# A decoder trunk on one core: SwiGLU's seven products with the tokens stationary and the weights moving 512 wide, the gated product turned by VectorE and on-chip transfers

## The chip, the cores and the metric

The kernel runs on one core of a Trainium2 chip. That core has five engines with instruction streams of their own: TensorE (PE: matrix products, with weight loads listed apart as PEld), VectorE (DVE), ScalarE (ACT), GpSimd (POOL) and SyncE (SP, which here only issues transfers). Each engine runs its stream strictly in order and waits on semaphores for the others. The metric is device time in microseconds for one execution of the whole program; lower is better.

## The reference

The program computes two layers over 512 tokens of width 1024: a recurrent layer, then an attention layer, each followed by a SwiGLU of hidden width 2816. Only the two SwiGLUs are touched by the change:

```
def rms_norm(x, g):
    y = x32 * lax.rsqrt(jnp.mean(x32 * x32, axis=-1, keepdims=True) + EPS)
    return y * g
def swiglu(h, w_in, w_out):
    g, u = jnp.split(h @ w_in, 2, axis=-1)
    return (jax.nn.silu(g) * u) @ w_out
...
h = h + swiglu(rms_norm(h, a_ffn_norm[i]), a_ffn_w_in[i], a_ffn_w_out[i])
```

## The kernel before, in words

Every float32 operand of a product is held as two parts, `hi` (its rounded value) and `lo` (the rest), and one product is three matmuls: hi by hi, hi by lo, lo by hi (`mm3`, lines 183 to 187). ScalarE makes `hi` by a cast, VectorE makes `lo` by a subtraction. So each weight tile costs one cast on ScalarE and one subtraction on VectorE before TensorE can use it; these pairs are called splits below.

The residual stream `h` lies with channels on the partitions and the 512 tokens along the free axis, as eight tiles. A SwiGLU (`swiglu`, line 574) has 22 blocks of 128 hidden units for the gate and 22 for the up projection. N_PLAIN = 1 pair of blocks goes through plain products, 24 matmuls a block. The other 20 blocks go in ten pairs, `q` = 1 to 10, and each pair is done in seven products in place of eight, after Winograd: the input is cut into two halves of the channels and two of the tokens, sums of these are made once (`B11`, `B21`, `B22`, `T1` to `T4`), sums of the weight parts are made for every pair (`GA`, `GB`, `S1` to `S4`, `UB`), and product "S2.T2" multiplies weight sum S2 with token sum T2. `S1` and `S3` are summed by an accumulating transfer that POOL issues behind one that SP issues (lines 634 and 636), `S2` and `S4` by VectorE (lines 644 and 647). Results collect in three PSUM accumulators: GA, S2, S3 and UB add into the one that GA begins, S4 into the one that S1 begins, and GB has its own.

A product of a pair is 24 matmuls: a 128x128 weight block is the stationary operand, 256 tokens move, and the result has hidden units on the partitions. `gate` and `results` (lines 700 to 709) multiply with the norm's factors, apply Silu, multiply gate and up, and split the gated block into `gh` and `gl`, four hidden blocks in one chunk. A chunk has two buffers. It is used by the out product (`out_block`, line 746): step "O" of the order is 24 matmuls, 512 tokens wide, and VectorE subtracts the result from `h` (line 752). The last six hidden blocks go through a loop at the end (line 765), where each of the eight output blocks is finished, and `after` makes the next stage's input from it.

TensorE's order is written by hand, as the lists PRODUCTS and LAST_PRODUCTS (lines 41 and 42). The other engines' streams are put in order when the program is built, by a scheduler. The class `Stream` (line 90) hands out the weight tiles, called pieces: `get(i)` returns piece `i` and has the splits of the next two pieces and the loads of the next four written into the program (`asp`, `al`, line 575). Split tiles `wh` and `wl` have three buffers each, so the cast for a piece must wait until TensorE has read the piece three before it for the last time. Tiles as loaded, `wr`, have two buffers; the raw tiles of the seven products have N_RAW = 7 between them.

```
        hi = self.pool.tile([128, 1024], F32R, name=f"wh{i}", tag="wh")
        lo = self.pool.tile([128, 1024], F32R, name=f"wl{i}", tag="wl")
...
                nc.scalar.copy(hi[:, c], r[:, c])
                kind = self.pieces[i][1]
```

In a pair's steady state the order is S1, S2, GB, O, S3, GA of the next pair, S4, O, UB. Between GA of a pair and its S2, which adds into the same accumulator after ScalarE has copied GA's result out (line 732), stand S4, O and UB of the pair before and S1 of its own.

Of the kernel before, what the change touches and what calls it, by code (L numbers as in the profile page):

```python
# [39 lines left out]
N_PLAIN = 1  # L40
LAST_PRODUCTS = ["S1.T1", "S2.T2", "GB.B21", "S3.T3", "O", "S4.B22", "UB.T4"]
PRODUCTS = ["S1.T1", "S2.T2", "GB.B21", "O", "S3.T3", "GA.B11", "S4.B22", "O", "UB.T4"]
# [47 lines left out]
class Stream:  # L90
# [31 lines left out]
    def _split(self, i):  # L122
# [4 lines left out]
        if self.pieces[i][0] is None:  # L127
            return [lambda: self.pieces[i][1](hi, lo)]
# [44 lines left out]
def trunk(tc, A, out):  # L173
# [29 lines left out]
    class Ffn:  # L203


        def __init__(self, wi, wo, gain):
            self.gain = gain
            self.wi, self.wo = A[wi], A[wo]
            self.split = None
            self.marks = {}  # L210
            self.steps = []
            for j in range(2 * N_PLAIN):
                self.steps += [("plain", j, b, add_pieces([self.wi[b]])) for b in (j, HB + j)]
            waiting = []

            def product(q, name):
                pieces.append((None, lambda hi, lo: self.split(q, name, hi, lo)))
                self.steps.append(("product", q, name, len(pieces) - 1))

            product(N_PLAIN, "GA.B11")  # L220
            for q in range(N_PLAIN, HB // 2):
                if q % 2 == 0:
                    waiting += [(q // 2 - 1, m) for m in range(0, 8, 2)]
                out = 1 if q > HB // 2 - 3 else 2
                for name in PRODUCTS if q + 1 < HB // 2 else LAST_PRODUCTS:
                    if name == "GA.B11":
                        if q + 1 < HB // 2:
                            product(q + 1, name)
                    elif name != "O":
                        product(q, name)  # L230
                    elif out and waiting:
                        c, m = waiting.pop(0)
                        w = self.wo[m:m + 2, :, 512 * c:512 * c + 512].rearrange("b q c -> q b c")
                        self.steps.append(("out", c, m, add_pieces([w])))
                        out -= 1
            self.gated = [s[3] for s in self.steps if s[0] == "out"][:2]
            self.last = [add_pieces([self.wo[m][:, 128 * (HB - 6):128 * HB]]) for m in range(8)]

        def half(self, u, q, k):

            b = (HB if u else 0) + 2 * q
            return self.wi[b:b + 2, :, 512 * k:512 * k + 512].rearrange("b q c -> q b c")
# [7 lines left out]
    with tc.tile_pool(name="keep", bufs=1) as kp, tc.tile_pool(name="wts", bufs=3) as wp, \  # L250
# [82 lines left out]
        def norm_rows(pool, r, tag="sq", bufs=1, copy=S.copy, hold=None, low=None):  # L333
# [12 lines left out]
            rb = pool.tile([128, T], F32, name="rb", bufs=1)  # L346
# [226 lines left out]

        def swiglu(fp, p, after):
            ws.asp, ws.al = 2, 4

            def chunk(extra=""):
                return [fp.tile([128, 4, T], F32R, name=n, tag=n, bufs=2) for n in ("gh", "gl")]
# [3 lines left out]
            for n in ("T1", "T2", "T3"):  # L582
                homes[n] = [fp.tile([128, 4, 256], F32R, name=n + x, bufs=1) for x in "hl"]
# [43 lines left out]
            def raw(q, n):  # L627
                raws[q, n] = fp.tile([128, 2, 512], F32, name=n, tag="raw", bufs=N_RAW)
                return raws[q, n]

            def fetch(q, n):
                r = raws[q, n]
                u, k = {"GA": (0, 0), "GB": (0, 1), "S1": (1, 0), "S3": (0, 0), "UB": (1, 1)}[n]
                a = nc.sync.dma_start(r, p.half(u, q, k))
                if n in ("S1", "S3"):
                    nc.gpsimd.dma_start(r, p.half(1, q, n == "S1"), accum_op=ALU.add)  # L636
                return a

            def split_weights(q, name, hi, lo):
                n = name[:2]  # L640
                with tc.high_priority():
                    if n == "S2":
                        raws[q, n] = raws[q, "S1"]
                        V.tensor_tensor(raws[q, n], raws[q, n], raws[q, "GA"], ALU.add)
                    elif n == "S4":
                        raws[q, n] = raws[q, "GB"]
                        V.tensor_tensor(raws[q, n], raws[q, n], raws[q, "S2"], ALU.add)
                    r = raws[q, n].rearrange("q b c -> q (b c)")
                    S.copy(hi, r)  # L649
                    p.marks[q, n] = V.tensor_tensor(lo, r, hi.bitcast(F32), ALU.subtract)  # L650

            p.split = split_weights
            chunks, rows, plain, acc = {}, [], {}, {}

            def store(q, w, c=slice(0, T)):
                n = min(q // 2, 4)
                if q == 10:
                    if 5 not in chunks:
                        chunks[5] = [fp.tile([128, 2, T], F32R, name=x, bufs=1) for x in ("ghx", "glx")]
                    dst = chunks[5]  # L660
                else:
                    if n not in chunks:
                        chunks[n] = chunk()
                    dst = [x[:, 2 * (q % 2):2 * (q % 2) + 2] for x in chunks[n]]
                halve(w, *(x[:, :, c] for x in dst))

            def pair_tile():
                return fp.tile([128, 2, T], F32, name="w", bufs=1)

            def temp(name="e"):  # L670
                return fp.tile([128, T], F32, name=name, tag="e", bufs=N_TMP)

            def plain_block(j, b, i):
# [6 lines left out]
                with tc.high_priority():  # L680
                    if b == 0:
                        p.r = norm_factors(fp)
                    elif b == 1:
                        rows.append(norm_rows(fp, p.r, "e", N_TMP, low=("e", N_TMP)))

            def plain_pair(j):
                if j == 0:
                    plain["w"] = pair_tile()
                g, w = temp("g"), plain["w"][:, j]
# [4 lines left out]
                if j:  # L694
                    store(0, plain["w"])

            def factor(half):
                return rows[0][:, 256 * half:256 * half + 256].unsqueeze(1).to_broadcast([128, 2, 256])

            def gate(q, half, ps, part):  # L700
                V.tensor_tensor(part, ps, part, ALU.add)
                V.tensor_tensor(halves(part), halves(part), factor(half), ALU.mult)
                S.activation(part, part, AF.Silu)
                V.tensor_tensor(halves(part), halves(part), factor(half), ALU.mult)  # L704

            def results(q, half, up, part):
                w = temp("w")
                p.mark = V.tensor_tensor(w, up, part, ALU.mult)
                store(q, halves(w), slice(256 * half, 256 * half + 256))

            def product(q, name, i):
                n, x = name.split(".")
                wh, wl = (t.rearrange("q (b k m) -> q b k m", b=2, k=4) for t in ws.get(i))
                begins = n in ("GA", "GB", "S1")
                if begins:
                    acc[n, q] = bank({"GA": "PT", "GB": "X", "S1": "OS"[q % 2]}[n])
# [7 lines left out]
                following = {"S1": ("GA", "S1"), "S2": ("GB",), "S4": ("S3", "UB")}.get(n, ())  # L724
                for r in following if q + 1 < HB // 2 else ():
                    raw(q + 1, r)
                    a = fetch(q + 1, r)
                    if r == "GB" and q == N_PLAIN:
                        ws.gate = {i: a for i in p.gated}
                if n in ("GA", "S2", "S3"):  # L730
                    part = acc["after " + n, q] = temp()
                    S.copy(part, ps)
                    if n == "S3":
                        V.tensor_tensor(part, acc["S1", q], part, ALU.add)  # L734
                elif n == "GB":
                    gate(q, 0, ps, acc["after GA", q])
                elif n == "S4":
                    gate(q, 1, ps, acc["after S2", q])
                    results(q, 1, acc["after S3", q], acc["after S2", q])
                elif n == "UB":  # L740
                    results(q, 0, ps, acc["after GA", q])

            def halves(t):
                return t.rearrange("q (b t) -> q b t", b=2)

            def out_block(c, m, i):
                wh, wl = (t.rearrange("q (b k m) -> q b k m", b=2, k=4) for t in ws.get(i))
                for b in range(2):
                    ps = bank("mm")
                    for k in range(4):  # L750
# [580 lines left out]
```

## Time and profile before

| | |
|---|---|
| Median of three runs | 1189.84 us (1189.64 to 1190.02) |
| The profiled execution's own time | 1190.41 us |
| Its span, first to last instruction | 1188.2 us |
| VectorE, ScalarE and POOL busy | 862.5, 623.3 and 166.2 us |
| First SwiGLU's seven products, about | 176 to 466 us of the span |
| Second SwiGLU's, about | 858 to 1151 us |
| HBM traffic | 164.99 MB read, 141 GB/s over the span |

The page gives for each engine its busy time, for groups of instructions their mean duration, and for idle time what ended it. A matmul row has its start and a duration; since matmuls are pipelined, the cost of one in a row of many is the distance between starts, not the duration. The lines on which the prediction rests are shown in it.

### The profile page before, as it was taken

Reading aid. Unit: us, or ns where it says so; the run is one execution under the profiler, and the core shown is the slowest. Engines: PE = TensorE matmul, PEld = TensorE weight load, DVE = VectorE, ACT = ScalarE, POOL = GpSimd, SP = SyncE. Lnnn points to the kernel's source line nnn. Section 1 sums busy time; section 2 is a strip of 40 time slices with the busy share of each in tenths; the row PEclk is TensorE's granted clock in tenths of the full one; section 3 lists DMA queues with packets and bytes.
Section 4 is the critical chain, followed back from the end, with each engine's and each line's share of the span. In section 5 each row is a group of like instructions: output and inputs, shape, how many; then the busy total and the mean of one; then the engine's idle time right before and its main releaser. Section 6 shows DMA issues by size and latency. Waiting matters only on the chain.

```text
span 1188.2 us, 18156 instructions
## 1 busy us (share of the span) xinstructions
PE 1172.6 (99%) x7083; PEld 1040.7 (88%) x7083; DVE 862.5 (73%) x1545; ACT 623.3 (52%) x897; POOL 166.2 (14%) x181
## 2 busy tenths in 40 slices
PE   9999999999999999999999999999999999999998
PEld 6787889999999999888888888898899999999996
DVE  8987689777777777977564677765997777777773
ACT  6796456444434344565555677655654344444441
POOL 4210010000000000010411334341100000000000
PEclk9999999999999999999999999999999999999999
DMA  7644367556655542433988657535685566556413
GB/s 242 148 108 107 106 201 196 150 146 160 158 144 147 155 103 73 117 101 93 225 182 179 138 119 175 106 72 124 194 205 152 142 159 155 149 147 154 101 54 111
DMA packets 71573, 169.30 MB, mean 142 GB/s; under 512 B 6080, under 2 KB 6976, under 8 KB 71488
## 3 DMA queue, kind: packets, MB, share of 16 engines
q1 hardware_dynamic: 52752, 122.36, 33.6%
q0 software_dynamic: 17584, 44.57, 22.1%
q10 hardware_dynamic: 1152, 1.23, 0.3%
q8 instruction: 55, 0.90, 0.3%
q14 instruction: 30, 0.25, 0.1%
HBM read 164.99 MB, written 2.10 MB: 141 GB/s over the span
## 4 chain that ended last, share of the span: by engine, by line
PE 87%; DVE 4%; issue 3%; ACT 2%; DMA 2%; POOL 1%; ACTq 0%; DVEq 0%; SPq 0%; POOLq 0%
PE ps L185 23%; PE ps L187 23%; PE ps L186 23%; PE ps L994 5%; PE ps L995 5%; PE ps L996 5%; DVE xc L475 1%; PE ps L1073 1%; PE ps L1160 1%; DMA wl<-in_w_in 1%; DMA GA<-in_f_in 1%; ACT pr L1146 0%; DVE xp L467 0%; DMA h<-in_x 0%; POOL xc L473 0%
## 5 line engine op out<-in xcount | busy, mean ns | idle before, releaser
L185 PE MATMUL ps<-xh,wh 128*128 128x256 f32 (+1 forms) x896 | 283.8, 317 | 2.8 <-DVE e L734 1.4
L187 PE MATMUL ps<-xh,wl 128*128 128x256 f32 (+1 forms) x896 | 281.0, 314 | 0.8 <-DMA wl<-in_w_in 0.8
L186 PE MATMUL ps<-xl,wh 128*128 128x256 f32 (+1 forms) x896 | 281.2, 314 | 0.1
L133 ACT CAST wh<-wr 128x1024 fp32r<-128x1024 f32 (+2 forms) x132 | 131.0, 993 | 122.2 <-PE ps L186 66.8
L185 PEld LDWEIGHTS ps<-xh,wh 128*128 128x128 f32 x896 | 170.6, 190 | 17.4 <-DVE e L734 5.7
L186 PEld LDWEIGHTS ps<-xl,wh 128*128 128x128 f32 x896 | 170.8, 191 | 11.2 <-DVE xl L304 0.7
L187 PEld LDWEIGHTS ps<-xh,wl 128*128 128x128 f32 x896 | 170.7, 191 | 11.2 <-DMA wl<-in_w_in 1.2
L636 POOL DMA_DIRECT2D S<-in_f_in x40 | 47.8, 1203 | 579.6 <-DVE e L704 203.7
L140 DVE TENSOR_TENSOR wl<-wr,wh 128x1024 fp32r<-128x1024 f32 (+3 forms) x89 | 100.2, 1128 | 35.8 <-ACT wh L133 35.5
L186 PE MATMUL ps<-gl,wh 128*128 128x512 f32 x320 | 125.0, 391 | 0.0
L185 PE MATMUL ps<-gh,wh 128*128 128x512 f32 x320 | 125.0, 391 | 0.0
L187 PE MATMUL ps<-gh,wl 128*128 128x512 f32 x320 | 124.5, 389 | 0.0
L649 ACT CAST wh<-S 128x1024 fp32r<-128x1024 f32 x60 | 62.8, 1047 | 76.9 <-PE ps L186 61.2
L650 DVE TENSOR_TENSOR wl<-S,wh 128x1024 fp32r<-128x1024 f32 x60 | 73.3, 1221 | 28.7 <-ACT wh L649 28.6
L994 PE MATMUL ps<-wh,xh 128*128 128x512 f32 x224 | 91.5, 408 | 0.0
L996 PE MATMUL ps<-wh,xl 128*128 128x512 f32 x224 | 87.7, 392 | 0.0
L995 PE MATMUL ps<-wl,xh 128*128 128x512 f32 x224 | 87.3, 390 | 0.0
L649 ACT CAST wh<-GB 128x1024 fp32r<-128x1024 f32 x40 | 42.1, 1052 | 83.6 <-PE ps L186 55.7
L187 PEld LDWEIGHTS ps<-gh,wl 128*128 128x128 f32 x320 | 60.1, 188 | 12.8
L185 PEld LDWEIGHTS ps<-gh,wh 128*128 128x128 f32 x320 | 60.2, 188 | 11.8
L186 PEld LDWEIGHTS ps<-gl,wh 128*128 128x128 f32 x320 | 60.2, 188 | 11.3
L752 DVE TENSOR_TENSOR h<-h,ps 128x512 f32<-128x512 f32 x64 | 43.5, 684 | 31.5 <-PE ps L187 31.5
(292 smaller groups left out, 2699.5 us busy)
## 6 DMA issues: line engine op xcount, KB each, us to landing
S<-in_f_in SPq DMA_DIRECT2D x40, 512.0 KB, 3.8
S<-in_f_in POOLq DMA_DIRECT2D x40, 512.0 KB, 7.9
wr<-in_f_out SPq DMA_DIRECT2D x32, 512.0 KB, 4.6
wr<-in_w_q SPq DMA_DIRECT2D x28, 512.0 KB, 6.4
wl<-in_w_q POOLq DMA_DIRECT2D x28, 512.0 KB, 7.2
GA<-in_f_in SPq DMA_DIRECT2D x20, 512.0 KB, 3.9
GB<-in_f_in SPq DMA_DIRECT2D x20, 512.0 KB, 6.4
UB<-in_f_in SPq DMA_DIRECT2D x20, 512.0 KB, 5.6
```

The lines of the kernel that those rows point to most:

```text
L133: nc.scalar.copy(hi[:, c], r[:, c])
L140: a = eng.tensor_tensor(lo[:, c], r[:, c], hi[:, c].bitcast(F32), ALU.subtract)
L185: PE.matmul(ps, wh, xh, start=first, stop=False, skip_group_check=on)
L186: PE.matmul(ps, wh, xl, start=False, stop=False, skip_group_check=on)
L187: PE.matmul(ps, wl, xh, start=False, stop=last, skip_group_check=on)
L636: nc.gpsimd.dma_start(r, p.half(1, q, n == "S1"), accum_op=ALU.add)
L649: S.copy(hi, r)
L650: p.marks[q, n] = V.tensor_tensor(lo, r, hi.bitcast(F32), ALU.subtract)
L752: V.tensor_tensor(h[m + b], h[m + b], ps, ALU.subtract)
L994: PE.matmul(ps[t], xh[k][:, r], wh[:, c], start=k == 0, stop=False)
L995: PE.matmul(ps[t], xh[k][:, r], wl[:, c], start=False, stop=False)
L996: PE.matmul(ps[t], xl[k][:, r], wh[:, c], start=False, stop=k == 7)
```

## The change

The same 20 hidden blocks per SwiGLU are now done in five groups of four blocks, `q` = 0 to 4, and the operands of the seven products change places: 128 tokens are the stationary operand, and 512 hidden units of the weights move. A product is now eight stationary tiles with three matmuls each, two halves `kk` of the channels, each a piece of its own, and two banks of PSUM, one for each 128 of its 256 tokens. So a result has tokens on the partitions. The norm's factor is then a number per partition, which Silu and `results` take as a scale; the multiplications with rows of factors are gone.

The out product still needs hidden units on the partitions. So `results` turns the gated product in blocks of 32x32 on VectorE into a tile `wt` (line 716), and `land` (line 718) puts the blocks in place with 16 transfers of 64 KB that SP issues, then splits the landed tile into `gh` and `gl`. The tokens come out in another order, and the subtraction from `h` goes through views that undo it (`by_time`, `in_turn`). The last group's gated product lands in the tiles of T1 and T2.

`gh` and `gl` have one buffer now. Each raw tile (1 MB for four blocks) has one buffer, and the fetch for the next group is written behind the last split that reads it. From the second group on, the sum `S1 += GA` comes behind GA's split, and `GB += S1` behind GB's; in the first group they are made before the splits of S2 and S4. The temporaries are twice as large, five in place of seven.

```
+MIDDLE = "S1.T1 GA.B11 S2.T2 O GB.B21 O S3.T3 O S4.B22 O UB.T4"
+ORDERS = ["GA.B11 GB.B21 O S1.T1 S2.T2 S3.T3 O S4.B22 UB.T4", MIDDLE, MIDDLE, MIDDLE,
+          "S1.T1 GA.B11 S2.T2 O GB.B21 S3.T3 O S4.B22 UB.T4 O O"]
...
+                S.copy(hi, r)
+                V.tensor_tensor(lo, r, hi.bitcast(F32), ALU.subtract)
+                if q and n in ("GA", "GB"):
+                    add(*{"GA": ("S1", "GA"), "GB": ("GB", "S1")}[n])
...
+            def gate(half, ps, part):
+                for i in range(2):
+                    V.tensor_tensor(part[:, i], ps[i], part[:, i], ALU.add)
+                    S.activation(part[:, i], part[:, i], AF.Silu, scale=p.r[:, 2 * half + i:2 * half + i + 1])
...
+                for i in range(2):
+                    j = 2 * half + i
+                    V.scalar_tensor_tensor(part[:, i], up[i], p.r[:, j:j + 1], part[:, i], ALU.mult, ALU.mult)
+                    p.mark = V.transpose(turned[q][:, :, j], part[:, i].rearrange("q (b i) -> q b i", i=32))
...
+            def land(q):
+                if q + 1 < len(ORDERS):
+                    hi, lo = chunks[q + 1] = chunk()
+                else:
+                    hi, lo = chunks[q + 1] = sums[:2]
+                src = turned.pop(q).rearrange("q (m b) t i -> q m b (t i)", b=4)
+                for a in range(4):
+                    for b in range(4):
+                        nc.sync.dma_start(lo[32 * b:32 * b + 32, :, 128 * a:128 * a + 128].bitcast(F32),
+                                          src[32 * a:32 * a + 32, :, b])
+                for m in range(4):
+                    S.copy(hi[:, m], lo[:, m].bitcast(F32))
+                    V.tensor_tensor(lo[:, m], lo[:, m].bitcast(F32), hi[:, m].bitcast(F32), ALU.subtract)
...
-                for b in range(2):
-                    c = slice(256 * b, 256 * b + 256)
-                    for k in range(4):
-                        mm3(ps[:, c], (wh[:, b, k], wl[:, b, k]), (xc[:, k], xd[:, k]),
-                            begins and b == k == 0, b == 1 and k == 3, not begins)
+                for kk in range(2):
+                    wh, wl = (t.rearrange("q (k c) -> q k c", k=2) for t in ws.get(first + kk))
+                    for k in range(2):
+                        for i in range(2):
+                            c = slice(128 * i, 128 * i + 128)
+                            mm3(ps[i], *[(x[:, 2 * kk + k, c], y[:, 2 * kk + k, c]) for x, y in [(xc, xd)]],
+                                (wh[:, k], wl[:, k]), begins and kk == k == 0, kk == k == 1, not begins)
...
+                    if c:
+                        V.tensor_tensor(by_time(x), by_time(x), in_turn(ps), ALU.subtract)
```

The streams of the other engines follow from this. ScalarE before, in a steady pair: piece 48 (`wh48`) is an out step's weights, `ps_2047` the accumulator that GA begins, and the line with `gh` splits a gated block that the out steps of the next pair but one will read.

```order
L649 CAST wh46_2151<-S1_1909 128x1024
L649 CAST wh47_2184<-GB_1940 128x1024
L308 CAST gh_2113<-w_2180 128x2x256
L133 CAST wh48_2218<-wr48_2149 128x1024
L649 CAST wh49_2250<-S3_2102 128x1024
L732 COPY e_2248<-ps_2047 128x512
L649 CAST wh50_2285<-GA_2213 128x1024
```

ScalarE after, in the third group, around its first out step (piece 68). Pieces 64 and 65 are GA, 66 and 67 are S2, 69 and 70 are GB; `ps_2476` and `ps_2477` are the two banks that GA and S2 share.

```order
L663 CAST wh67_2496<-S1_2115 128x1024
L749 COPY e_2512<-ps_2476 128x512
L133 CAST wh68_2515<-wr68_2478 128x1024
L749 COPY e_2512<-ps_2477 128x512
L663 CAST wh69_2533<-GB_2268 128x1024
L749 COPY e_2550<-ps_2476 128x512
L663 CAST wh70_2553<-GB_2268 128x1024
L749 COPY e_2550<-ps_2477 128x512
L729 CAST gh_2411<-gl_2412 128x512 x4
L133 CAST wh71_2593<-wr71_2531 128x1024
```

The casts that make `gh` for the out step stand behind the cast of GB's second piece and the last copy of S2's result, and the out step reads them at once; before, they were made a pair earlier. GA's two copies have the cast of piece 68 between them.

VectorE after, at the same place; `gl` is the other half of what the out step reads, and the two lines with `ps_2563` and `ps_2577` take its results.

```order
L140 TENSOR_TENSOR wl68_2516<-wr68_2478,wh68_2515 128x1024
L664 TENSOR_TENSOR wl69_2534<-GB_2268,wh69_2533 128x1024
L656 TENSOR_TENSOR GB_2268<-GB_2268,S1_2115 128x4x256
L664 TENSOR_TENSOR wl70_2554<-GB_2268,wh70_2553 128x1024
L656 TENSOR_TENSOR GB_2268<-GB_2268,S1_2115 128x4x256
L730 TENSOR_TENSOR gl_2412<-gl_2412,gh_2411 128x512 x4
L772 TENSOR_TENSOR h0_64<-h0_64,ps_2563 128x4x4x32
L772 TENSOR_TENSOR h1_65<-h1_65,ps_2577 128x4x4x32
```

The four subtractions for `gl` stand behind both splits of GB and both sums `GB += S1`. In the first group VectorE has this order at the out step, whose four output blocks use the banks 1692, 1700, 1708 and 1716; 1708 is the same memory as bank 1651, GB's second, and 1716 the same as 1692.

```order
L664 TENSOR_TENSOR wl33_1669<-S1_1384,wh33_1668 128x1024
L705 TENSOR_TENSOR e_1637<-ps_1650,e_1637 128x512
L656 TENSOR_TENSOR S1_1384<-S1_1384,GA_1378 128x4x256
L664 TENSOR_TENSOR wl34_1689<-S1_1384,wh34_1688 128x1024
L656 TENSOR_TENSOR GB_1381<-GB_1381,S1_1384 128x4x256
L656 TENSOR_TENSOR S1_1384<-S1_1384,GA_1378 128x4x256
L705 TENSOR_TENSOR e_1637<-ps_1651,e_1637 128x512
L656 TENSOR_TENSOR GB_1381<-GB_1381,S1_1384 128x4x256
L774 TENSOR_TENSOR h0_64<-h0_64,ps_1692 128x512
```

Between the two reads of GB's banks (line 705) stand a split and three sums of 1024 elements, and the first read of an out bank comes last.

More of the change, by code (lines that the diff above doesn't have):

```diff
@@ L209, in __init__ @@
             self.split = None
-            self.marks = {}
             self.steps = []
-            for j in range(2 * N_PLAIN):
+            for j in range(2):
                 self.steps += [("plain", j, b, add_pieces([self.wi[b]])) for b in (j, HB + j)]
[L214 to L241, printed above, removed]
+            for q, names in enumerate(ORDERS):
+                waiting = list(range(0, 8, 2 if q else 4))
+                for name in names.split():
+                    if name == "O":
+                        m = waiting.pop(0)
+                        if q:
+                            w = self.wo[m:m + 2, :, 512 * q - 256:512 * q + 256]
+                        else:
+                            w = self.wo[m:m + 4, :, :256]
+                        self.steps.append(("out", q, m, add_pieces([w.rearrange("b q c -> q b c")])))
+                    else:
+                        first = len(pieces)
+                        for kk in range(2):
+                            pieces.append((None, lambda hi, lo, *a: self.split(*a, hi, lo), q, name, kk))
+                        self.steps.append(("product", q, name, first))
@@ L242, in half, with part @@
+            self.last = [add_pieces([self.wo[m][:, 128 * (HB - 4):128 * HB]]) for m in range(8)]
+        def part(self, u, q, k, i):
+            b = (HB if u else 0) + 2 + 4 * q + 2 * i
             return self.wi[b:b + 2, :, 512 * k:512 * k + 512].rearrange("b q c -> q b c")
@@ L345, in norm_rows @@
             PE.matmul(ps, ones_r, dl, start=False, stop=True)
-            rb = pool.tile([128, T], F32, name="rb", bufs=1)
+            rb = (keep or pool).tile([128, T], F32, name="rb", bufs=1)
             copy(rb, ps)
@@ L652, in swiglu @@
-            p.split = split_weights
[L653 to L665, printed above, removed]
@@ L673, in plain_block, with pair_tile @@
+            p.split = split_weights
+            rows, plain, acc = [], {}, {}
+            def pair_tile(name="e"):
+                return temps.tile([128, 2, T], F32, name=name)
             def plain_block(j, b, i):
@@ L694, in plain_pair @@
                 if j:
[L695 to L704, printed above, removed]
@@ L706, in results @@
-            def results(q, half, up, part):
[L707 to L711, printed above, removed]
+                    chunks[0] = chunk()
+                    halve(plain["w"], *(x[:, 2:4] for x in chunks[0]))
+            def gate(half, ps, part):
+                for i in range(2):
+                    V.tensor_tensor(part[:, i], ps[i], part[:, i], ALU.add)
+                    S.activation(part[:, i], part[:, i], AF.Silu, scale=p.r[:, 2 * half + i:2 * half + i + 1])
```

161 lines of the change are left out of this document (86 added, 75 removed).

## The prediction
> **What bounds the kernel now.** First the page's head, its busy times and its chain, then TensorE's waits, then the window of one steady pair.
>
> ```profile
> span 1188.2 us, 18156 instructions
> PE 1172.6 (99%) x7083; PEld 1040.7 (88%) x7083; DVE 862.5 (73%) x1545; ACT 623.3 (52%) x897; POOL 166.2 (14%) x181
> PE 87%; DVE 4%; issue 3%; ACT 2%; DMA 2%; POOL 1%; ACTq 0%; DVEq 0%; SPq 0%; POOLq 0%
> ...
> PE ps L372 <- DVE warm L369: 1.4, 1, 1.4
> PE ps L185 <- DVE e L734: 1.4, 3, 0.7
> ...
> 282.00:313.30 31.30, 31.25 (x218) 29.16 (x216) 22.48 (x27) 13.21 (x16) 2.39 (x2) 1.00 0.58 152
> ```
>
> TensorE is busy for 99% of the span, its longest sums of waits (total, times, longest) are 1.4 us, and in a pair's window of 31.30 us it works 31.25 at a granted clock of 1.00, while VectorE has 22.48 and ScalarE 13.21. So the kernel is bound by TensorE's number of matmuls and their pitch; a change pays if it lowers that product, and costs every moment that it makes TensorE wait.
>
> **The pitch.** Rows of the timeline: start, duration, line. The distance of starts counts.
>
> ```profile
> 442.09 0.28 PE L185 MATMUL ps<-xh,wh 128*128 128x256 f32 x1
> ...
> 447.85 0.28 PE L185 MATMUL ps<-T2h,wh 128*128 128x256 f32 x1
> ...
> 511.42 0.39 PE L994 MATMUL ps<-wh,xh 128*128 128x512 f32 x1
> ...
> 522.99 0.39 PE L994 MATMUL ps<-wh,xh 128*128 128x512 f32 x1
> ```
>
> The first two are 48 starts apart: 5.76 / 48 = 0.120 us for 256 columns. The last two are 51 starts apart: 11.57 / 51 = 0.2269 for 512, in the projections that already hold tokens stationary and move weights, the form that the change uses. Before, 2 SwiGLUs x 10 pairs x 7 products x 24 = 3360 matmuls at 0.120 take 403.2; after, 2 x 5 x 7 x 24 = 1680 at 0.2269 take 381.2. **Term 1: -22.0.** The out, plain and last products keep their matmuls in number and width.
>
> ```profile
> 281.90 0.28 PE L187 MATMUL ps<-xh,wl 128*128 128x256 f32 x1
> 282.23 0.39 PE L185 MATMUL ps<-xh,wh 128*128 128x256 f32 x1
> ...
> 509.24 0.49 PE L994 MATMUL ps<-wh,xh 128*128 128x512 f32 x1
> 509.57 0.40 PE L995 MATMUL ps<-wl,xh 128*128 128x512 f32 x1
> ...
> 510.73 0.40 PE L994 MATMUL ps<-wh,xh 128*128 128x512 f32 x1
> ```
>
> At a pair's start there is a break, 0.33 in place of 0.12, so 0.21; 20 of them are 4. With half as many groups it may halve: **term 2: -2** (bounds 0 and -4). The other rows show a restart after a wait: 0.33 in place of 0.227 at first, so 0.1 on top of each new wait, and five matmuls later a pitch of 0.232 (1.16 / 5).
>
> [...]
>
> **What the new order makes TensorE wait for, groups 2 to 5 of each SwiGLU.** I set t = 0 at the start of S1. A product takes 24 x 0.2269 = 5.44: S1 0, GA 5.44, S2 10.88, O 16.32.
>
> ```profile
> L649 ACT CAST wh<-GB 128x1024 fp32r<-128x1024 f32 x40 | 42.1, 1052 | 83.6 <-PE ps L186 55.7 <-issue 27.4 <-ACT wh L649 0.4
> L732 ACT COPY e<-ps 128x512 f32<-128x512 f32 x60 | 34.8, 581 | 0.0
> L308 ACT CAST gh<-w 128x512 fp32r<-128x512 f32 x36 | 22.2, 618 | 40.2 <-DVE w L708 40.0
> L650 DVE TENSOR_TENSOR wl<-GB,wh 128x1024 fp32r<-128x1024 f32 x40 | 48.9, 1224 | 8.4 <-ACT wh L649 8.4
> L647 DVE TENSOR_TENSOR GB<-GB,S 128x1024 f32<-128x1024 f32 x20 | 24.4, 1219 | 0.0
> L309 DVE TENSOR_TENSOR gl<-w,gh 128x512 fp32r<-128x512 f32 x36 | 24.7, 685 | 0.0
> ...
> 299.43 1.05 ACT L649 CAST wh<-S 128x1024 fp32r<-128x1024 f32 x1 [1.83 <-PE ps L186]
> 300.38 0.58 ACT L732 COPY e<-ps 128x512 f32<-128x512 f32 x1
> ...
> 296.50 1.22 DVE L647 TENSOR_TENSOR GB<-GB,S 128x1024 f32<-128x1024 f32 x1
> 297.63 1.22 DVE L140 TENSOR_TENSOR wl<-wr,wh 128x1024 fp32r<-128x1024 f32 x1
> ...
> 152.34 0.39 PE L187 MATMUL ps<-hgh,wl 128*128 128x512 f32 x1
> 152.59 1.05 ACT L133 CAST wh<-wr 128x1024 fp32r<-128x1024 f32 x1 [3.24 <-issue]
> ```
>
> Back to back the cast has a pitch of 0.95 and the 1024-wide VectorE sum or subtraction 1.13. A cast starts 0.25 after the start of the last matmul that reads its buffer.
>
> Wait A: S2 adds into GA's two banks, so it needs both copies by ScalarE. Between them stands the cast of piece 68, whose buffer GA's last matmul frees: cast from 11.1 to 12.07, second copy to 12.65. S2 writes the second bank with its fourth matmul, due at 11.56. That is 1.1; its first matmul waits about 0.1 for the first copy. Together **1.2**.
>
> Wait B: the out step is then due at 17.5. Its `gh` and `gl` stand behind the second piece of GB. That cast waits for the buffer that S2's last piece frees (17.65), and runs to 18.7; VectorE subtracts from 18.74 (1.13), adds `GB += S1` (1.13), and then makes `gl`, 0.69: 21.7. ScalarE's copy of S2 (0.58) and first `gh` (0.62) end at 19.9 and hide beside that. The later three `gl` follow 0.6 apart, within the 0.68 of three matmuls. So TensorE waits from 17.5 to 21.6: **4.1**. GB, queued behind, loses nothing more: its splits are made in that time. The mean of one group is 1.2 + 4.1 = 5.3, and 0.1 for restarts is inside the rounding of A. **Term 3: 8 groups x 5.3 = +42.4.**
>
> **Is the landing later than that?**
>
> ```profile
> 156.25 0.89 SPq L634 DMA_DIRECT2D S<-in_f_in  x2
> ...
> out_h<-h SPq DMA_DIRECT2D x1, 128.0 KB, 1.8
> vh<-ph POOLq DMA_DIRECT2D x8, 64.0 KB, 4.8
> vl<-pl POOLq DMA_DIRECT2D x8, 64.0 KB, 7.2
> ```
>
> SP issues a transfer in 0.45. The 16 of `land` start at about 5.9, behind the fetch for the next GA (8.6 in the second group, where more fetches stand ahead), so the last is issued at 13 to 15.8. Landing took 1.8 for 128 KB from SP and 4.8 to 7.2 for 64 KB from POOL. I take 2.2, near the row of the same queue: 15.2 to 18. `gh` is due on ScalarE at 19.2, so the landing is hidden; at 7.2 it lands at 20.3 to 23, which is a rival. The turns on VectorE are not in the trace. Nearest are a 256-wide sum and a 512-wide scan:
>
> ```profile
> L591 DVE TENSOR_TENSOR gh<-h 128x256 f32<-128x256 f32 x16 | 5.7, 417 | 0.0
> L517 DVE TENSOR_TENSOR_SCAN gated<-rate,gated 128x512 f32<-128x512 f32 x8 | 9.5, 1212 | 0.0
> ```
>
> 0.42 to 1.21; I take 0.69 as for other 512-wide operations. 2 x 5 x 4 = 40 turns are 17 to 48 us on VectorE, which has 31.30 - 22.48 = 8.8 us free in each of 20 pairs, and the multiplications with factor rows go. At 1.21 a group's last two turns delay `land` by 1, inside its slack: 0 either way.
>
> **The first group, each SwiGLU.** GB is followed by an out step with four blocks. VectorE's second read of GB's banks stands behind a split and three sums; it is done 5.7 after GB's end, and the third out block, in the same bank, is due at 2.7: 3.0. The fourth needs the first block's subtraction from `h`, one later: 0.4. S2 straight before S3, with the copies of S2 between, costs 1.2 as in A; GA of the next group waits 1.1 for VectorE's second read of UB. **Term 4: 5.7 x 2 = +11.4.**
>
> **The last products** need the last group's landed tile.
>
> ```profile
> 478.73 0.22 DVE L850 TENSOR_SCALAR rtmp<-rtmp 128x128 f32<-128x128 f32 x1
> 478.98 0.23 DVE L851 TENSOR_SCALAR rtmp<-rtmp 128x128 f32<-128x128 f32 x1
> ```
>
> After UB two out steps cover 10.88. The last turn stands behind the first out block's subtraction, so SP issues from 4.1 after UB's end, 16 x 0.45 = 7.2, lands 2.2 later at 13.5, and a cast and a subtraction (1.27) end at 14.8: **3.9** for the second SwiGLU. In the first, rotary's chain (some 25 VectorE operations 0.25 apart, and two Sin on ScalarE) stands ahead of the landed tile's casts: ready at 19.2, so **8.3**. **Term 5: +12.2.**
>
> **The start.** 7.5 MB of raw tiles load during the plain products.
>
> ```profile
> 164.00:168.00 4.00, 4.00 (x19) 3.33 (x18) 3.69 (x10) 1.05 (x1) 0.00 (x0) 1.00 1.04 285
> 168.00:172.00 4.00, 4.00 (x19) 3.29 (x18) 3.86 (x9) 2.60 (x4) 0.00 (x0) 1.00 1.10 263
> ```
>
> The DMA share is 1.0 there already, at 263 to 285 GB/s; from 156, the S1 sum is in at about 180 and due at 184. I cost it at 0; if it is not covered, 3 to 5 per SwiGLU.
>
> **Sum.** -22.0 - 2 + 42.4 + 11.4 + 12.2 = +42.0. The profiled execution took 1190.4, its span 1188.2, 0.6 over the median of 1189.84. 1190.4 + 42.0 - 0.6 = **1232**.
>
> **Rivals.** (1) The landing is slow, 7.2 as in POOL's row: in the worst place `gl` is ready at 23.9 in place of 21.7, 8 x 2.2 = 18, and 5 more in each tail, 10: 1260. For: that row; against: SP's own rows. (2) The waits are half hidden: ScalarE or VectorE run earlier than I place them, so B is 2 and A 0.5, 8 x 2.8 = 22 less: 1210. (3) Width buys little. If every matmul ran at the 0.232 that follows a restart, term 1 would be 389.8 - 403.2 = -13.4: 1241. Against: the 51 starts above. [...] (4) The other sign, one mechanism: at the out steps VectorE and ScalarE run ahead of my placing, in the 8.8 us that VectorE has free per pair, by a lead L, and each of the 12 waits of terms 3 to 5 shrinks by it. It decides from 66 - 12 L = 24, L = 3.5; with a lead of 6, only 2.3 of the longest wait is left, 1168. For: both engines are free for long in the window above. Against: the order of the streams, where `gh` and `gl` stand behind GB's second piece, whose buffer S2's own last matmul frees; no free time moves that. (5) Gains and waits cancel; no single mechanism gives it.
>
> **How the numbers follow.** Forecast 1232 (1220 to 1246): 0.62. Landing late, 1246 to 1270: 0.14. Waits half hidden, 1200 to 1220: 0.12. Width buys little: 0.05. Faster, 1160 to 1185: 0.05. Same: 0.02. To hold 8 in 10, the range takes the forecast, part of the half-hidden and part of the late case: 1214 to 1258. A measurement tells 0.2% (2.4 us) from no change. Faster: 0.05; same: 0.02; slower: 0.93.
>
> **What would show it.** Term 1: tokens-stationary matmuls start 0.227 apart. A: in each group one wait of about 1 at S2's fourth matmul, for a copy's tile. B: one of about 4 at the first out step, for `gl`; were it for S2's accumulator or DMA instead, B's reason fails. Term 5: a long wait ahead of the last products, twice as long in the first SwiGLU. `land`: the time from issue to landing near 2. TensorE's busy time falls by about 24 while its idle time rises to 70 or more. If idle stays below 30, the prediction is wrong.

## The result and the profile after

The changed kernel takes 1252.89 us (median of 4 runs, 1249.94 to 1255.06) against 1189.93 (4 runs): 1.0524 times as long, 95% interval 1.0500 to 1.0548. The forecast was 1232 with a range of 1214 to 1258: the sign and the range held, and the forecast itself fell 21 us short. The kernel before was run again beside the experiments: its median is 1191.33 beside 1, 2, 4 and 5 below, and 1191.16 beside 3, 6 and 7; their ratios are to these.

The page of the changed kernel, its head, its clock by slices and its chain; then TensorE's waits (waiter, releaser: total us, times, longest):

```profile
span 1251.0 us, 15052 instructions
...
PE 1180.6 (94%) x5403; PEld 966.0 (77%) x5403; DVE 853.3 (68%) x1525; ACT 626.9 (50%) x901; POOL 166.6 (13%) x181
...
PEclk9999999999898989899999999999999999989898
...
PE 76%; DVE 9%; ACT 6%; issue 3%; DMA 3%; SPq 2%; POOL 1%; DVEq 0%; ACTq 0%; POOLq 0%
```

```profile
PE ps L185 <- ACT gh L729: 18.1, 8, 2.8
PE ps L185 <- ACT T L729: 13.7, 2, 7.4
PE ps L186 <- DVE gl L730: 11.0, 7, 1.6
PE ps L185 <- ACT e L749: 6.5, 10, 0.6
PE ps L185 <- DVE e L705: 5.5, 2, 2.8
PE ps L185 <- DVE e L715: 1.9, 2, 1.0
```

Two things stand there. The waits are the ones that were forecast, each at its place: `gh` and `gl` ahead of the first out step, T1 and T2 (`T`) ahead of the last products, ScalarE's copies (`e`, line 749) ahead of the second bank, VectorE's reads of GB's and UB's banks. And PE's busy time, which should have fallen by 24, rose by 8, while the granted clock shows eights where before, on the line below, it was nine throughout. TensorE's matmuls became slower somewhere.

```profile
PEclk9999999999999999999999999999999999999999
```

One first out step in TensorE's timeline (start, duration), and the windows around it (start:end length, busy times, then granted clock, DMA share, GB/s):

```profile
316.00 0.39 PE L187 MATMUL ps<-wh,T 128*128 128x512 f32 x1
318.53 0.50 PE L185 MATMUL ps<-gh,wh 128*128 128x512 f32 x1 [2.14 <-ACT gh L729]
320.65 0.80 PE L186 MATMUL ps<-gl,wh 128*128 128x512 f32 x1 [1.62 <-DVE gl L730]
321.24 0.63 PE L187 MATMUL ps<-gh,wl 128*128 128x512 f32 x1
...
326.35 0.39 PE L187 MATMUL ps<-gh,wl 128*128 128x512 f32 x1
326.58 0.40 PE L185 MATMUL ps<-gh,wh 128*128 128x512 f32 x1
```

```profile
310.00:318.50 8.50, 5.75 (x24) 4.06 (x23) 4.67 (x4) 5.00 (x8) 0.00 (x0) 1.00 0.46 133
321.00:326.00 5.00, 5.00 (x13) 3.89 (x13) 1.65 (x4) 0.00 (x0) 1.82 (x2) 0.50 0.88 314
326.50:330.00 3.50, 3.50 (x17) 2.86 (x16) 0.96 (x2) 1.06 (x1) 0.10 (x1) 1.00 1.04 173
```

The out step was due 0.23 after 316.00. It comes at 318.53, and its second matmul at 320.65: 2.30 + 1.89 = 4.19 us of wait (the brackets count from the end of the matmul before and so show a little less). Then the starts stand 0.43 apart in place of 0.227, at a granted clock of 0.50, until 326.35. TensorE has lost another 2.8 us without waiting for anything.

What ScalarE and VectorE did meanwhile:

```profile
316.43 1.04 ACT L663 CAST wh<-GB 128x1024 fp32r<-128x1024 f32 x1
317.38 0.58 ACT L749 COPY e<-ps 128x512 f32<-128x512 f32 x1
317.86 2.18 ACT L729 CAST gh<-gl 128x512 fp32r<-128x512 f32 x4
```

```profile
317.50 1.22 DVE L664 TENSOR_TENSOR wl<-GB,wh 128x1024 fp32r<-128x1024 f32 x1 [0.23 <-ACT wh L663]
318.76 1.23 DVE L656 TENSOR_TENSOR GB<-GB,S 128x1024 f32<-128x1024 f32 x1
319.91 2.49 DVE L730 TENSOR_TENSOR gl<-gl,gh 128x512 fp32r<-128x512 f32 x4
```

`gh` follows a copy without a break and `gl` follows `GB += S1` without one: both are held by the order of their engines, not by the landing, whose last transfer is in at 316.31. In the second group of each SwiGLU it is the landing that lets `gh` start (last transfers in at 251.23 and 966.07, casts at 251.54 and 966.14); TensorE's idle time is the same there (2.83 + 0.92 in place of 2.14 + 1.62), because `gl`, behind `GB += S1`, ends the wait.

**The account.** Read off the starts (distance less 0.227, with the slower matmuls of a restart), the eight first out steps wait 34.5 in all, the copies between GA and S2 7.4, the first groups 10.9, the last products 8.2 and 6.5: 67.5. Over windows of half a microsecond, the time at half clock, weighted with PE's busy time in it, lost 24.9. The span grew by 1251.0 - 1188.2 = 62.8, so 29.6 were saved. The sum is good to some 2 us. It leaves out 0.27 in each of ten groups, 2.7 in all: the product that follows the copies starts its first two matmuls 0.39 and 0.34 after the ones before them, where experiment 5, without that wait, has 0.227. And counted by the starts (0.427 apart in place of 0.227) the half clock costs 23.3.

### The profile page after: what moved, and what is told of

The parts are those of the page before. It is cut to its first block, busy times and chain, and to the rows that moved or that the text cites. A ratio compares the mean times of both kernels' runs of the same rounds, so it can differ in the third digit from the quotient of the medians.

```text
span 1251.0 us, 15052 instructions
## 1 busy us (share of the span) xinstructions
PE 1180.6 (94%) x5403; PEld 966.0 (77%) x5403; DVE 853.3 (68%) x1525; ACT 626.9 (50%) x901; POOL 166.6 (13%) x181
## 4 chain that ended last, share of the span: by engine, by line
PE 76%; DVE 9%; ACT 6%; issue 3%; DMA 3%; SPq 2%; POOL 1%; DVEq 0%; ACTq 0%; POOLq 0%
PE ps L186 20%; PE ps L187 20%; PE ps L185 20%; PE ps L1012 5%; PE ps L1013 5%; PE ps L1014 5%; SPq L726 2%; DVE wl L664 2%; ACT wh L663 1%; ACT wh L133 1%; DVE S L656 1%; DVE xc L466 1%; PE ps L1091 1%; DVE e L715 1%; PE ps L1178 1%
## 5 line engine op out<-in xcount | busy, mean ns | idle before, releaser
L185 PE MATMUL ps<-wh,xh 128*128 128x512 f32 x320 | 124.7, 390 | 1.9 <-DVE e L715 1.9
L187 PE MATMUL ps<-wh,xl 128*128 128x512 f32 x320 | 124.5, 389 | 0.0
L186 PE MATMUL ps<-wl,xh 128*128 128x512 f32 x320 | 124.5, 389 | 0.0
L140 DVE TENSOR_TENSOR wl<-wr,wh 128x1024 fp32r<-128x1024 f32 (+2 forms) x93 | 100.7, 1084 | 30.0 <-ACT wh L133 29.8
L187 PE MATMUL ps<-gh,wl 128*128 128x512 f32 x288 | 119.9, 416 | 0.0
L185 PE MATMUL ps<-wh,T 128*128 128x512 f32 x240 | 95.8, 399 | 6.5 <-ACT e L749 6.5
L185 PE MATMUL ps<-xh,wh 128*128 128x512 f32 x256 | 101.0, 396 | 0.5 <-ACT xh L294 0.5
L187 PE MATMUL ps<-xh,wl 128*128 128x512 f32 x256 | 100.0, 391 | 0.8 <-DMA wl<-in_w_in 0.8
L186 PE MATMUL ps<-xl,wh 128*128 128x512 f32 x256 | 100.1, 391 | 0.1
L186 PE MATMUL ps<-wl,T 128*128 128x512 f32 x240 | 93.6, 390 | 0.0
L187 PE MATMUL ps<-wh,T 128*128 128x512 f32 x240 | 93.4, 389 | 0.0
L1012 PE MATMUL ps<-wh,xh 128*128 128x512 f32 x224 | 91.5, 408 | 0.0
L1014 PE MATMUL ps<-wh,xl 128*128 128x512 f32 x224 | 87.7, 392 | 0.0
L1013 PE MATMUL ps<-wl,xh 128*128 128x512 f32 x224 | 87.3, 390 | 0.0
```

Of the source, the lines that this page charges most:

```text
L140: a = eng.tensor_tensor(lo[:, c], r[:, c], hi[:, c].bitcast(F32), ALU.subtract)
L185: PE.matmul(ps, wh, xh, start=first, stop=False, skip_group_check=on)
L186: PE.matmul(ps, wh, xl, start=False, stop=False, skip_group_check=on)
L187: PE.matmul(ps, wl, xh, start=False, stop=last, skip_group_check=on)
L1012: PE.matmul(ps[t], xh[k][:, r], wh[:, c], start=k == 0, stop=False)
L1013: PE.matmul(ps[t], xh[k][:, r], wl[:, c], start=False, stop=False)
```

## The experiments

**1. The first out step behind GB** (groups 2 to 5). It moves one step of TensorE and so gives ScalarE and VectorE 5.4 us for `gh` and `gl`.

```diff
-MIDDLE = "S1.T1 GA.B11 S2.T2 O GB.B21 O S3.T3 O S4.B22 O UB.T4"
+MIDDLE = "S1.T1 GA.B11 S2.T2 GB.B21 O O S3.T3 O S4.B22 O UB.T4"
...
-          "S1.T1 GA.B11 S2.T2 O GB.B21 S3.T3 O S4.B22 UB.T4 O O"]
+          "S1.T1 GA.B11 S2.T2 GB.B21 O S3.T3 O S4.B22 UB.T4 O O"]
```

> The first out step of groups 2 to 5 moves behind GB, nothing else. Theory (the wait of 4.2 us ahead of the first out step is the order of ScalarE and VectorE, and the half clock of about 2.4 us that follows is its consequence): the wait shrinks from 4.2 to at most 1.3 in each of the 8 groups, the clock stays at 1.00 there, and the time falls by 8 x (3 to 4) + 19 = 43 to 51, to 1202 to 1210. Rival a (the landing of the turned tile is late, and the out step waits for that): TensorE waits for the same moment, 5.4 us later, so the wait is gone too, but the casts for gh start when the last transfer lands, not when ScalarE is free. Rival b (the clock falls because of the 512-wide moving weights, whatever the waits): the half clock stays, and the time falls by 25 to 32 only, to 1221 to 1228.

Measured: 1211.44 us, ratio to before 1.0170 (1.0143 to 1.0197), so 41 less than the change, a little short of the expected 43 to 51. TensorE's waits in it:

```profile
PE ps L185 <- ACT T L729: 13.8, 2, 7.4
PE ps L185 <- ACT e L749: 6.6, 10, 0.7
PE ps L185 <- DVE e L705: 5.5, 2, 2.8
PE ps L186 <- DVE gl L730: 3.4, 4, 1.1
```

No wait for `gh` is left, and four for `gl`: both second groups, where three of the four casts for `gh` fall behind S3's first cast. The other six groups wait for less than 0.1 at their out steps and have a clock of 1.00. The casts for `gh` follow ScalarE's work ahead of them without a break, so the rival of a late landing falls too. Of the half-clock loss 12.4 stay (mean granted clock 0.987 against 0.975 in the changed kernel), at the first groups, one of the second groups, the last products and one place in the attention. The rival by which the 512-wide form drags the clock falls: the form is the same, and the clock is 1.00 wherever the wait is gone.

**2. The same waits, filled** with 16 matmuls that TensorE can run at once; the first real matmul overwrites their result.

```diff
                     ps = bank("mm")
+                    if c and m == b == 0:
+                        for _ in range(16):
+                            PE.matmul(ps, xhs[:, 0, 0:128], xhs[:, 1], start=True, stop=True)
```

> Ahead of the first out step of groups 2 to 5 TensorE gets 16 matmuls of 512 columns whose result is overwritten (16 x 0.227 = 3.6 us); all waits of the other engines stay. Theory (the clock is halved because TensorE stands idle for some 4 us): the out step still begins at the same time, but no half clock follows, so 8 groups gain 1.4 to 3.0 each, 19 in all: 1234. Rival b (the clock falls because of the form of the products or the burst of transfers, not because of the idle time): 1253 or more, with the half clock at the same places.

Measured: 1234.63 us (ratio 1.0364, 1.0344 to 1.0385), 18.3 less than the change with 8 x 16 matmuls more. Its timeline at a first out step, and the windows there:

```profile
312.35 3.79 PE L770 MATMUL ps<-xh 128*128 128x512 f32 x16
315.98 0.39 PE L185 MATMUL ps<-gh,wh 128*128 128x512 f32 x1
316.78 0.50 PE L186 MATMUL ps<-gl,wh 128*128 128x512 f32 x1 [0.41 <-DVE gl L730]
```

```profile
316.00:321.00 5.00, 4.59 (x20) 3.49 (x19) 3.22 (x6) 0.17 (x1) 0.56 (x1) 1.00 0.70 252
321.00:326.00 5.00, 5.00 (x24) 4.14 (x23) 1.91 (x2) 2.00 (x2) 1.86 (x2) 1.00 0.92 188
```

The second matmul of the out step comes as late as before (4.4 us after the step's turn), the transfers run as before (DMA share 0.70 and 0.92, against 0.75 and 0.90 at the same place of the changed kernel), and the clock stays at 1.00. Summed as above the half clock costs 5.5 in place of 24.9 (mean granted clock 0.993), all of it at the last products. So the half clock here comes with TensorE's idle time: 0.50 behind the empty wait, 1.00 behind the filled one; summed in the changed kernel, its price at the eight places is 19.3 us.

**3. How long an idle stretch must be.** The same kernel with 6 and with 10 filling matmuls.

> As the kernel with 16 filling matmuls, with 6 of them (1.36 us), so that about 2.8 us of idle time are left ahead of the first out step. It asks how long an idle stretch has to be. If the clock is halved by idle time as such, in proportion, a part of the half clock stays: about 1245. If it takes a stretch of some 3 us or more, the half clock is gone as with 16 and the time is 1235. If any stretch over 2 us is enough, the half clock stays in all 8 groups: 1253.

> As before with 10 filling matmuls (2.27 us), so that about 1.9 us of idle time are left. Where the limit lies above 2 us, no half clock: 1235; where it lies below, as with 6: 1245 to 1253.

Measured: 1240.22 and 1235.65 us (one run each). The first out step with 6, and then with 10:

```profile
316.40 1.52 PE L770 MATMUL ps<-xh 128*128 128x512 f32 x6
318.70 0.49 PE L185 MATMUL ps<-gh,wh 128*128 128x512 f32 x1 [0.78 <-ACT gh L729]
320.83 0.50 PE L186 MATMUL ps<-gl,wh 128*128 128x512 f32 x1 [1.63 <-DVE gl L730]
```

```profile
312.78 2.43 PE L770 MATMUL ps<-xh 128*128 128x512 f32 x10
315.09 0.50 PE L185 MATMUL ps<-gh,wh 128*128 128x512 f32 x1
317.21 0.50 PE L186 MATMUL ps<-gl,wh 128*128 128x512 f32 x1 [1.62 <-DVE gl L730]
```

With 10, 1.62 of idle time are left in the middle groups and 1.50 in the second ones, and none of the 8 groups loses its clock. With 6, 2.4 are left in each group (0.78 + 1.63 here), and three of 8 do. Unfilled, 3.8 are left (2.14 + 1.62 with one matmul between, in the middle groups), and all 8 do. The first groups' wait of 2.70 to 2.75 took the clock in one of the two SwiGLUs in the changed kernel, in the one with 6 and in the one with 10. Between 1.6 and 3.8 us these runs show no sharp limit. The time with 10 came out at the 1235 that was expected without half clock. That with 6 lies between the 1235 and the 1245 in proportion, because in it three groups had half clock and five had none.

What else decides was not shown. In the changed kernel the stretches at half clock last 3.41 or 6.83 us, and full clock lasts 44.37, 58.03, 61.44 or 64.85 between two of them in one SwiGLU, which are 13, 17, 18 and 19 times 3.413. In the kernel with 6 half clock begins at 190.24, 255.09, 497.44, 961.65 and 1094.77, also whole multiples of 3.413 apart, and lasts 3.42, 6.83 or 10.24. So the times were cut into such steps and TensorE's idle time was counted in each. Here are the step with the first group's wait in the changed kernel's first SwiGLU, and the two steps between which the same wait of its second SwiGLU is divided (the first busy time is TensorE's):

```profile
189.80:193.21 3.41, 1.25 (x5) 1.05 (x6) 3.41 (x5) 0.73 (x1) 0.00 (x0) 1.00 0.20 44
903.19:906.60 3.41, 2.34 (x11) 1.61 (x9) 3.41 (x4) 1.39 (x2) 0.00 (x0) 1.00 0.02 8
906.60:910.01 3.41, 1.69 (x7) 1.09 (x7) 3.41 (x5) 0.73 (x1) 0.00 (x0) 1.00 0.29 103
```

The step with 3.41 - 1.25 = 2.16 of idle time is followed by half clock, those with 1.07 and 1.72 are not. At the first groups' wait, steps with 1.97 (with 6) and 2.15 (with 10) were followed by half clock, and those with 1.90 (with 6) and 1.85 (with 10) were not. But with 6 a step with 1.63, at the second group of the first SwiGLU, was followed by half clock too, and one with 1.63 in a middle group of the second was not. So the idle time in a step does not decide alone. This was read off the traces afterwards; no run was made to test it.

**4. The last landing on two queues**: the last group's 16 transfers divided between SP and ScalarE.

```diff
-                        nc.sync.dma_start(lo[32 * b:32 * b + 32, :, 128 * a:128 * a + 128].bitcast(F32),
+                        (nc.scalar if q + 1 == len(ORDERS) and b % 2 else nc.sync).dma_start(lo[32 * b:32 * b + 32, :, 128 * a:128 * a + 128].bitcast(F32),
```

> Only the last group's 16 landing transfers are divided between SP and ScalarE's queue. Theory (the wait ahead of the last products is bound in the second SwiGLU by SP's issuing, 16 x 0.65 us; in the first by rotary's chain, which ends at about the same time): the wait falls from 6.5 to about 1.5 in the second SwiGLU with its half clock gone (2), and by less than 1 in the first: 1245 to 1247. Rival (the wait is VectorE's and ScalarE's work ahead of the landing, or the transfer itself): no change in either, 1253.

Measured: 1244.59 us (ratio 1.0448, 1.0425 to 1.0471). In the changed kernel SP's issuing in a middle group and ahead of the first SwiGLU's last products, the landing times, and ScalarE's first cast of the last landed tile of the second SwiGLU read

```profile
304.59 10.26 SPq L726 DMA_DIRECT2D gl<-wt  x16
...
496.76 10.38 SPq L726 DMA_DIRECT2D T<-wt  x16
...
gl<-wt SPq DMA_DIRECT2D x128, 64.0 KB, 2.0
...
1222.44 2.18 ACT L729 CAST T<-T 128x512 fp32r<-128x512 f32 x4 [5.26 <-DMA T<-wt]
```

16 issues take 10.3 us, 0.65 each; a landing takes 2.0. With two queues the second SwiGLU's wait went from 6.5 to 1.8 and its half clock went, as expected. The first's went from 8.2 to 5.3, where less than 1 was expected: VectorE's stream has rotary's chain behind the split of the landed tile there (line 863 at 507.32, the split at 504.91), so rotary no longer stood in front. What held the cast until 504.26 is the landing: ScalarE issues the last two of its eight transfers behind a cast of an out step's weights (499.75), and the last one, issued at 500.41, is in at 504.08. The theory that left the first SwiGLU's wait to rotary's chain is not tested by this run, since the chain moved.

**5. Another order of the same products**, with GA first, S2 two products after it, the out steps between the products that share an accumulator, and three of them behind UB in the last group. `S1 += GA` comes behind S1's split and the fetch of the next GA with it.

```diff
-MIDDLE = "S1.T1 GA.B11 S2.T2 O GB.B21 O S3.T3 O S4.B22 O UB.T4"
-ORDERS = ["GA.B11 GB.B21 O S1.T1 S2.T2 S3.T3 O S4.B22 UB.T4", MIDDLE, MIDDLE, MIDDLE,
-          "S1.T1 GA.B11 S2.T2 O GB.B21 S3.T3 O S4.B22 UB.T4 O O"]
+MIDDLE = "GA.B11 S1.T1 S2.T2 GB.B21 O S3.T3 O S4.B22 O UB.T4 O"
+ORDERS = ["GA.B11 S1.T1 S2.T2 GB.B21 S3.T3 O S4.B22 UB.T4 O", MIDDLE, MIDDLE, MIDDLE,
+          "GA.B11 S1.T1 S2.T2 GB.B21 S3.T3 O S4.B22 UB.T4 O O O"]
...
-                    if q and n in ("GA", "GB"):
-                        add(*{"GA": ("S1", "GA"), "GB": ("GB", "S1")}[n])
+                    if q and n in ("S1", "GB"):
+                        add(*{"S1": ("S1", "GA"), "GB": ("GB", "S1")}[n])
...
-                    gone = {"GA": "GA", "GB": "S1", "S4": "GB"} if q else {"S2": "GA", "S4": "S1 GB"}
+                    gone = {"S1": "GA", "GB": "S1", "S4": "GB"} if q else {"S2": "GA", "S4": "S1 GB"}
...
-            for n in ("GA", "GB", "S1", "S3", "UB"):
+            for n in ("GA", "S1", "GB", "S3", "UB"):
                 fetch(0, n)
```

> The same products and the same 512-wide form in another order: GA, S1, S2, GB, then out steps between the others, one of them behind UB; the sum S1 += GA follows S1's split; in the last group three out steps stand behind UB. Theory (all that was lost are waits of the order and their half clock; the narrower count of matmuls saves 24 to 27): waits of A and B go in all groups, the first groups lose 0 to 1, the last products wait 1 to 3: 1190 - 27 + 5 = 1168, range 1163 to 1180. Rival b (the form drags the clock): 1190 or more. Rival (the landing is too slow for any order): waits of 2 or more ahead of the out steps remain.

Measured: 1171.31 us, faster than before by a ratio of 0.9836 (0.9820 to 0.9852). Its longest waits:

```profile
PE ps L185 <- ACT T L729: 4.4, 2, 2.7
PE ps L363 <- DVE warm L360: 1.4, 1, 1.4
PE ps L186 <- DVE wl L664: 1.3, 3, 0.6
```

All the waits of the middle groups are gone. One group's eleven steps take 11 x 5.44 = 59.84, where two pairs took 2 x 31.30 = 62.60: 2.76 saved in each group, 27.6 in ten.

**6. That order with the last landing on two queues.**

> The changed order with the last group's 16 transfers divided between SP's and ScalarE's queue. Theory (the waits of 3.5 and 2 us left ahead of the last products in the new order are bound by the issuing of 16 transfers on one queue): both go below 1 us, the one remaining half clock (1.6) goes too: 1171 - 6 = 1165, 1163 to 1167. Rival (the first SwiGLU's wait is rotary's chain): the second SwiGLU's goes, the first's stays: 1169.

Measured: 1163.31 us, ratio to before 0.9776 (0.9756 to 0.9797). The page's head and the longest waits:

```profile
span 1161.7 us, 15050 instructions
...
PE 1146.9 (99%) x5403; PEld 951.1 (82%) x5403; DVE 850.1 (73%) x1525; ACT 623.9 (54%) x901; POOL 165.5 (14%) x181
```

```profile
PE ps L186 <- DVE wl L664: 1.7, 4, 0.5
PE ps L363 <- DVE warm L360: 1.4, 1, 1.4
```

TensorE is busy for 99% again, with 25.7 us of work less than before, and the mean granted clock is 1.000 (0.975 in the changed kernel). Both waits ahead of the last products are gone. That does not tell SP's issuing from rotary's chain in the first SwiGLU: with two queues VectorE has the chain behind the landed tile's split again (line 863 at 468.73, the split at 465.12), while in experiment 5, with one queue, the chain held ScalarE's cast until 468.04, after the last landing at 467.26.

**7. All four out steps of the last group behind UB**, on top of 6.

```diff
-          "GA.B11 S1.T1 S2.T2 GB.B21 S3.T3 O S4.B22 UB.T4 O O O"]
+          "GA.B11 S1.T1 S2.T2 GB.B21 S3.T3 S4.B22 UB.T4 O O O O"]
```

> As the one before, and all four out steps of the last group stand behind UB, none between S3 and S4. Theory: S4 adds into the accumulator that S1 began and S3's result reads, so it waits about 1.3 for a copy and an addition in each SwiGLU, and the cover behind UB grows by 5.4, which is more than is needed: 1165 + 2 x 1.3 less what is left of the waits ahead of the last products, 1166 to 1168; not faster than the one before by more than 1.

Measured: 1172.37 us (ratio 0.9840, 0.9826 to 0.9853), worse than expected. S4 waits for the addition of S3's result:

```profile
PE ps L185 <- DVE e L751: 4.2, 4, 1.4
...
PE ps L1012 <- DVE h L803: 1.4, 1, 1.4
```

It waits once for each bank, not once, and the projection behind the first SwiGLU waits for VectorE as well: 5.6 us in the list for an expected 2.6. The profiled executions differ by 6.3 (spans of 1168.0 and 1161.7), the medians by 9.1. The other three executions have spans of 1170.4 to 1171.2 at a mean granted clock of 0.997 to 0.998, where the profiled one has 1.000, so a part of the rest goes with a lower clock.

## Why the prediction was right in sign and short in size

**The pitch (term 1) and the breaks (term 2): right, slightly low.** Tokens-stationary matmuls run at 0.227. The break at a pair's start is not halved but gone, so term 2 was at its bound, 4 in place of 2, and an out step takes 5.44 in place of 5.47 between products of its own width. The whole saving is 27.6 by the clean groups of experiment 5, against 24; the 2 more in the sum of the account are not assigned.

**The rivals.** The late landing falls with `gh` following a copy at once and 2.0 us to land; little gain from the width falls with the 27.6; waits half hidden and VectorE's lead (the rival on the other side) fall with 67.5 measured for 66.0. The range held by luck: its upper part was there for a late landing, which added nothing to the groups' waits, and it was filled by the half clock, which the prediction does not have.

**Wait B: right.** 34.5 measured against 32.8; experiment 1 shows that it is the place of the out step in the order, since moving that step alone removes it. **Wait A: right**, 7.4 at the second bank and 2.2 (8 x 0.27) ahead of it, for the first copy, against 9.6.

**The first groups: right**, 10.9 and another 0.5 for the first copies against 11.4, at the places named. **The last products: 14.7 against 12.2.** The term that was mis-sized is SP's issuing: a landing transfer takes 0.65 to issue, not the 0.45 of the row it was taken from. Experiment 4 shows it for the second SwiGLU; in the first, 8.2 against 8.3, the last transfer was in at 508.60 and rotary's chain held ScalarE's cast until 509.99, so that the size came out right by rotary, but only the last 1.4 are rotary's alone.

**The turn and the landing: right.** Forty turns at 697 ns against 0.69 chosen, 2.0 us to land against 2.2, both hidden in the middle groups. In the second groups the slower issuing, 16 x 0.2 = 3.2 more, used up the slack that the prediction had there.

**The step that failed** is the sentence on restarts: "so 0.1 on top of each new wait". Before, no wait in the two SwiGLUs was longer than 0.7, and a restart costs 0.1 after such a one. After the 3.8 of idle time ahead of a first out step it costs 1.4 to 3.0. The prediction's range of the waits stopped at the moment when TensorE began again. That one omission is 24.9; with 67.5 - 66.0 = 1.5 more of waits and 29.6 - 24.0 = 5.6 more saved it gives the 20.8 that the forecast lay low. The forecast for idle time, a rise to 70 or more, held (PE's idle time went from 15.6 to 70.4), while that for PE's busy time failed for the same reason.

## What to carry to other kernels

A wait on TensorE had two prices here, its own length and, in some cases from 2.4 us on and at all eight waits of 3.8 us, 3.41 to 10.24 us at half clock behind it; add the second when you cost a change, and look at the granted clock in windows, not only at the waits. Where a change makes the steps fewer and longer, redo the order of the steps with it: here one letter's place in a list was worth 41 us, and the same wider products went from 5% slower to 2.2% faster. For a chain of many small transfers count the issuing on one queue (here 16 x 0.65 us) before the landing (2.0).

## What the runs showed of the hardware

The half clock came in stretches of 3.41 or 6.83 us in the changed kernel, and of 3.42, 6.83 or 10.24 in the kernel with 6 filling matmuls; within each execution they began whole multiples of 3.413 us apart. Of the idle times ahead of the first out step, those of 1.50 to 1.62 us took the clock in none of eight groups, those of 2.4 in three and those of 3.8 in all eight; the first groups' 2.70 to 2.75 took it in three of six cases. Behind the 3.8 us came one stretch of 3.41 us in three groups and one of 6.83 in five.

With a matmul counted as 0.227 us of work for 512 columns, and narrower ones in proportion, the 11 steps at full clock that half clock followed in the changed kernel lack 2.28 to 3.41 us of work, and all others after its first 20 us at most 2.02; in the kernel before, with a mean granted clock of 1.000, the steps lack at most 2.07. These two kernels do not fix a limit: with 6 filling matmuls half clock followed a step that lacks 2.03 and did not follow one that lacks 2.16. In the changed kernel the steps at half clock that another followed, with 0.43 for a matmul, lack 0.99 to 3.41, the others at most 0.72. Matmuls without a use, which only keep TensorE busy during a wait that stays as long, saved 18 us.
